# Modulation pieces over two feed-forward groups, and where a chunk's transposes stand

## The chip, the cores and the metric

The kernel runs on one core of one Trainium2 chip. A core has a matrix engine (TensorE, in the profile PE, its weight loads PEld), VectorE (DVE), ScalarE (ACT), GpSimd (POOL) and SyncE (SP), which here issues all DMAs. The metric is the device time of one execution in microseconds (us).

## What the reference computes

Two blocks of layers over 512 tokens of width 1024, all in float32. The first block has two layers; each also carries 256 context tokens, which the second layer (`last` in the kernel) no longer needs as output:

```python
mod = c_act @ w_mod[l] + b_mod[l]        # six rows: sh1, sc1, g1, sh2, sc2, g2; modc for the context
px = (rmsnorm(x, norm1_g[l]) * (1.0 + sc1) + sh1) @ w_in[l] + b_in[l]
...
x = x + g1 * (y_x @ w_out[l])
x = x + g2 * swiglu(rmsnorm(x, norm2_g[l]) * (1.0 + sc2) + sh2, w_gu[l], w_down[l])
```

The second block has two attention layers. After each mixer: `x = layer_norm(ALPHA * x + h)`, then `x = x + sigmoid(x @ ple_w_gate[i]) * (p[i] @ ple_w_proj[i])`.

## The kernel before

**Precision and tiles.** Every large product is made of three matmuls: an operand is split into a rounded part `hi` and a rest `lo`, and hi*hi, hi*lo and lo*hi are summed in PSUM. `wblock` (L154) loads a weight block in two halves into `raw`, copies each to `hi` on ACT and subtracts on DVE for `lo`; `hi` and `lo` have three buffers each, `raw` three. Activations are kept both by token (a chunk is 128 tokens, `xt[c]`) and transposed, features on partitions, as a pair `Hh`, `Hl`.

**A chunk's way into H.** `scaled` (L380) multiplies a chunk by its 1/rms; `finish_T` (L349) makes eight TensorE transposes in two groups of four, applies a scale and a shift per feature (first group on ACT, second on DVE), copies to `Hh` on ACT and subtracts for `Hl` (first group on DVE, second on POOL). `to_T` (L393) does the same without scale and shift, with both subtractions on DVE.

**What sets the order.** The code is one long program; `Pending` (L53) holds functions with a chunk's number as key, so that their instructions are written later than the place where they are added: `keep(n)` runs all but the newest n, `upto(key)` all up to a key. `Lane` (L32) holds generators, `pump(n)` runs n of their steps, `drain` all. When the program is built, a scheduler orders each engine's instructions; the place in the code counts as priority among those that are ready, and a tile's instructions wait for a free buffer of its pool.

**Layer, after the mixer** (L984 to L1005): for each chunk c in turn the output projection in its quarters n = 2 and 3 (48 matmuls of 256 columns), the residual (`resid`), the sum of squares, and with n = 3 the pending list's `keep(1)`, `scaled`, and `finish_T(c)` added to the list. With n = 3 of the last chunk but one the first gate-and-up block gu[0] is loaded, in layer 1 with the last chunk gu[1] too.

**Feed-forward** (L1010 on): 22 blocks of 128 hidden features in groups of 4, 6, 6 and 6. For each block gate and up are 96 matmuls; after a group, its down projection (`wide`, L225) adds to the residual in two halves of 512 columns, each from two weight blocks. Chunks 0 to 3 sum in banks of the PSUM pool "mm" (four), chunk 4 in "md" (one bank), chunk 5 in "tr" (three). Block 0 goes by 256 columns of tokens (`fm_pair`, L196, in layer 0; `fm_pairs`, L206, blocks 0 and 1 in layer 1) and calls `upto` between them, as does the first projection of the second attention (L1635).

**Modulation pieces.** `mod_gen` (L271) computes one of the six rows of `mod` as a generator: four steps that each load 1 MB of `w_mod` into the one buffer `wm` and issue 16 matmuls of 32 weight columns (TensorE rows `md<-wm,cact`), which sum in a bank of "md", and a fifth step that reads the bank (DVE `mb`), and transposes or stores the row. In layer 0 five such generators are added in block 0 (L1035 on): the rows g2 of this layer and sh1, sc1, g1, sc2 of the next; in layer 1 one, g2. Each block pumps 3 steps in layer 0 and 1 in layer 1, and after group 0 the lane is drained.

**After an attention** (`post_attention`, L1293): `wide` with the output weights; in its second half each chunk is finished in turn, normalised, and `finish_T(c)` is added after `keep(1)`. Then `embed_gate` (L1337) runs `wide` with the gate weights, whose `pre` calls `upto(c + 1)` ahead of each chunk's step (L1339). After the first attention its `done_a` (L1609) transposes each finished chunk into HB for the second.

Of the kernel before, what the change touches and what calls it, by code (L numbers as in the profile page):

```python
# [70 lines left out]
def emit(ctx, tc, a, out):  # L71
# [12 lines left out]
    def close(p):  # L84
        p[0].__exit__(None, None, None)
# [68 lines left out]
    def wblock(src, nk, n, into=None):  # L154
        hi, lo = into or (T(wp, [128, nk, n], t, F32R, bufs=3) for t in ("hi", "lo"))
        h = (nk + 1) // 2
        for k0, k1 in ((0, h), (h, nk)):
            raw = T(wp, [128, k1 - k0, n], "raw", bufs=3)
            ld(raw, src[:, k0 * n:k1 * n].rearrange("p (k n) -> p k n", n=n))
            hs = hi[:, k0:k1, :]  # L160
            act(hs, raw, AF.Copy)
            tt(lo[:, k0:k1, :], raw, hs.bitcast(F32), SUB)
        return hi, lo
# [32 lines left out]
    def fm_pair(wb, H, segs):  # L196

        pss = [[mmt()[:, 0:n] for (_, n) in segs] for _ in range(2)]
        for i, (o, n) in enumerate(segs):
            for q in range(0, n, 256):  # L200
                pend.upto((o + q) // 128 + 3)
                for m in range(2):
                    fm_into([pss[m][i][:, q:q + 256]], wb, 128 * m, H, [(o + q, 256)])
        return pss
# [125 lines left out]
    def mcol(l, what, r):  # L330
        t = modc[l][what]
        return lambda kc: t[:, kc % 2, kc // 2, r:r + 1]
# [4 lines left out]
    modl = Lane()  # L337
# [42 lines left out]
    def scaled(pool, xt, rs):  # L380

        h = [T(pool, [128, 512], "xs", bufs=4) for _ in range(2)]
        ts(h[0], xt[:, 0:512], rs, MUL)
        act(h[1], xt[:, 512:1024], AF.Copy, scale=rs)
        return lambda kc: h[kc // 4][:, 128 * (kc % 4):128 * (kc % 4) + 128]
# [486 lines left out]
    def layer(l, H1, hside, oside, x_in, nn, mix_mods, ffn_mods):  # L872
# [111 lines left out]
        for n, c in order:  # L984
                if n not in wbo:
                    wbo[n] = wblock(a["w_out"][l, n], 8, 256)
                if (n, c) == (3, chs[-2]):
                    gu[0] = wblock(a["w_gu"][l, 0], 8, 256)
                if last and (n, c) == (3, chs[-1]):
                    gu[1] = wblock(a["w_gu"][l, 1], 8, 256)  # L990
                wb = wbo[n]
                if n or c >= ne:
                    ps = mmt()[:, 0:256]
                    out_proj((Yh, Yl), wb, c, ps)
                else:
                    ps = early["ps"][:, c, :]
                if n == 3:
                    pend.keep(1)
                resid(OP, c, n, ps, gb[c // 4])
                if n == 0:  # L1000
                    ss[c] = sst()
                sq_part(OP, ss[c], xt[c], n)
                if n == 3:
                    xn = scaled(NP, xt[c], rms(ss[c]))
                    pend.add(c, lambda xn=xn, c=c: finish_T(NP, xn, H2, 128 * c, mcol(l, SC2, c // 4),  # L1005
                                                            mcol(l, SH2, c // 4)))
        close(YP)
        close(OP)

# [3 lines left out]
        for gi, grp in enumerate(GROUPS):  # L1013
            acts = {}
            for jj in grp:
                if jj in gu:
                    wb = gu[jj]
                else:
                    with behind("AV" if jj == 1 else ""):
                        wb = wblock(a["w_gu"][l, jj], 8, 256)  # L1020
                ah = T(FP, [128, TT_], "ah", F32R, bufs=6)
                al = T(FP, [128, TT_], "al", F32R, bufs=6)
                if jj == 0 and last:
                    both = fm_pairs([wb, gu[1]], H2, 2)
                    pg, pu = both[0]
                elif jj == 0:
                    pg, pu = fm_pair(wb, H2, segs)
                elif jj == 1 and last:
                    pg, pu = both[1]
                else:  # L1030
                    pg = fm(wb, 0, H2, segs)
                    pu = fm(wb, 128, H2, segs)
                if jj == 0:
                    close(NP)
                    MP = opened("mp", oside)  # L1035
                    for m in ffn_mods:
                        modl.add(mod_gen(*m, pool=MP))
                modl.pump(1 if last else 3)
                sg = T(FP, [128, TT_], "sg", bufs=2)
                for p, (o, n) in zip(pg, segs):  # L1040
                    act(sg[:, o:o + n], p, AF.Sigmoid)
                    tt(sg[:, o:o + n], p, sg[:, o:o + n], MUL)
                for p, (o, n) in zip(pu, segs):
                    tt(sg[:, o:o + n], p, sg[:, o:o + n], MUL)
                split(ah, al, sg)
                acts[jj] = (ah, al)
            if gi == 0:
                modl.drain()
                close(MP)
                for q in range(1 if last else 2):  # L1050
                    t = T(FP, [128, D], "g2", bufs=2)
                    bcast_row(t, gd[l][1, q])
                    g2.append(t)
            lastg = gi == len(GROUPS) - 1
            if lastg:
                close(H2p)
                H1n = nn["open"](oside, FP)

            def down(c, n2, ps):
                if lastg and n2 == 1:  # L1060
                    pend.keep(1)
                for n in (2 * n2, 2 * n2 + 1):
                    resid(FP, c, n, ps[:, 256 * (n % 2):256 * (n % 2) + 256], g2[c // 4])
                    if lastg:
                        if n == 0:
                            ss[c] = sst()
                        sq_part(FP, ss[c], xt[c], n)
                        if n == 3:
                            nn["chunk"](H1n, c, xt[c], ss[c])

            wide(a["w_d4"][l] if gi == 0 else a["w_d6"][l, gi - 1], len(grp) // 2,
                 lambda c, k: [t[:, 128 * c:128 * c + 128] for t in acts[grp[k]]], chs,
                 lambda c: mmt() if c < 4 else (mdt, trt)[c - 4](), down, by_chunk=lastg)
# [219 lines left out]
    def post_attention(i, Y, w_out, xin, sideh, first=None):  # L1293
        HP = opened("hp", sideh)
        H = halloc(HP, 512)
        PO = opened("po", sideh)
        lg = T(PO, [128, D], "lg")
        lb = T(PO, [128, D], "lb")
        bcast_row(lg, a["ln_g"][i])
        bcast_row(lb, a["ln_b"][i])  # L1300
        xt, bst = {}, {}
        for c in range(4):
            xt[c] = T(w6, [128, D], "w")
            ld(xt[c], xin(c))

        def use(c, n2, ps):
            for n in (2 * n2, 2 * n2 + 1):
                sl = slice(256 * n, 256 * n + 256)
                stt(xt[c][:, sl], xt[c][:, sl], ALPHA, ps[:, 256 * (n % 2):256 * (n % 2) + 256], MUL, ADD)
                if n == 0:  # L1310
                    bst[c] = T(S2, [128, 4, 6], "lst", bufs=4)
                V.bn_stats(out=bst[c][:, n, :], in_=xt[c][:, sl])
                if n == 3:
                    pend.keep(1)
                    mv = T(sm, [128, 2], "mv")
                    V.bn_aggr(out=mv, in_=bst[c])
                    rs = T(sm, [128, 1], "rs")
                    rstd_of(rs, mv[:, 1:2], LN_EPS)
                    nb = T(sm, [128, 1], "nb")
                    stt(nb, mv[:, 0:1], -1.0, rs, MUL, MUL)  # L1320
                    ts(xt[c][:, 0:512], xt[c][:, 0:512], mv[:, 0:1], SUB, rs, MUL)
                    act(xt[c][:, 512:1024], xt[c][:, 512:1024], AF.Identity, scale=rs, bias=nb)
                    pend.add(c, lambda c=c: finish_T(PO, blocks(xt[c]), H, 128 * c, lcol(1 + i), lcol(3 + i)))

        wide(w_out, 4, lambda c, k: [t[:, 128 * c:128 * c + 128] for t in Y[k]], range(4), bank4, use, None, None, first)

        def affine(c):
            with behind("G"):
                tt(xt[c], xt[c], lg, MUL, e=G)
            tt(xt[c], xt[c], lb, ADD)  # L1330

        return HP, H, PO, xt, affine
# [276 lines left out]
    def done_a(c, n, t):  # L1609
        if n == 3:  # L1610
            if not HB:
                HB.extend(T(HBp, [128, 8, 512], t, F32R, bufs=1) for t in ("Hh", "Hl"))
            ld(x4[c], t)
            to_T(lambda kc: t[:, 128 * kc:128 * kc + 128], HB, 128 * c)

    embed_gate(0, H, PO, xt, affine, done_a, early)
    close(PO)
# [270 lines left out]
```

## Time and profile before

| what | value |
|---|---|
| median of 3 runs | 2688.26 us (2686.65 to 2691.68) |
| profiled execution | 2693.03 us |
| its span, first to last instruction | 2691.3 us |
| TensorE busy in the span | 2570.1 us, 95% |
| DVE, ACT, POOL busy | 1330.6, 971.6, 574.2 us |
| mean granted TensorE clock | 0.979 of full speed |

The profiled execution is the one that every row below comes from; its own time is its span and 1.7 us around it. A busy TensorE is not TensorE at its peak, since matmuls overlap in the records. Waits that matter are those of the engine that is busy nearly always, so the stretches to look for are those where TensorE is not.

### The profile page before, as it was taken

Reading aid. Unit: us, or ns where it says so; the run is one execution under the profiler, and the core shown is the slowest. Engines: PE = TensorE matmul, PEld = TensorE weight load, DVE = VectorE, ACT = ScalarE, POOL = GpSimd, SP = SyncE. Lnnn points to the kernel's source line nnn. Section 1 sums busy time; section 2 is a strip of 40 time slices with the busy share of each in tenths; the row PEclk is TensorE's granted clock in tenths of the full one; section 3 lists DMA queues with packets and bytes.
Section 4 is the critical chain, followed back from the end, with each engine's and each line's share of the span. In section 5 each row is a group of like instructions: output and inputs, shape, how many; then the busy total and the mean of one; then the engine's idle time right before and its main releaser. Section 6 shows DMA issues by size and latency. Waiting matters only on the chain.

```text
span 2691.3 us, 39898 instructions
## 1 busy us (share of the span) xinstructions
PE 2570.1 (95%) x15408; PEld 2168.1 (81%) x15408; DVE 1330.6 (49%) x2858; ACT 971.6 (36%) x2034; POOL 574.2 (21%) x614
## 2 busy tenths in 40 slices
PE   7999989859999999999999999999999999989998
PEld 5888788638888888887888888888888888768776
DVE  5675654123232325656634434444454545665666
ACT  3324534012121115344522222433434345434743
POOL 1175531010110204015411211311111211021112
PEclk9999999969999999999999999999999999999999
DMA  8321643541221213225543323343444444524452
GB/s 299 129 71 54 185 157 124 182 147 61 65 68 58 73 53 117 71 78 160 179 132 104 102 85 97 119 119 94 124 126 124 128 122 131 172 86 135 119 165 63
DMA packets 132287, 314.77 MB, mean 117 GB/s; under 512 B 18784, under 2 KB 49088, under 8 KB 132096
## 3 DMA queue, kind: packets, MB, share of 16 engines
q1 hardware_dynamic: 132096, 312.20, 37.0%
q8 instruction: 122, 2.00, 0.3%
q14 instruction: 69, 0.57, 0.1%
HBM read 272.02 MB, written 13.89 MB: 106 GB/s over the span
## 4 chain that ended last, share of the span: by engine, by line
PE 84%; DMA 5%; DVE 4%; ACT 3%; POOL 2%; issue 2%; SPq 0%; DVEq 0%; POOLq 0%; ACTq 0%
PE mm L138 70%; PE md L138 6%; PE tr L138 5%; DMA wm<-in_w_mod_dram 3%; PE tr L1271 1%; POOL w L124 1%; DMA t<-mwd 1%; ACT t L121 1%; DVE lo L124 1%; DVE t L124 1%; ACT hi L121 0%; DVE w L124 0%; DMA g<-gd 0%; POOL t L124 0%; ACT sb L121 0%
## 5 line engine op out<-in xcount | busy, mean ns | idle before, releaser
L138 PE MATMUL mm<-Hh,hi 128*128 128x512 f32 (+1 forms) x2208 | 800.2, 363 | 3.5 <-ACT hi L121 3.3
L138 PE MATMUL mm<-Hl,hi 128*128 128x512 f32 (+1 forms) x2208 | 773.4, 361 | 1.6 <-DVE rv L131 1.3
L138 PE MATMUL mm<-Hh,lo 128*128 128x512 f32 (+1 forms) x2208 | 713.4, 361 | 1.4 <-DVE lo L124 1.4
L121 ACT ACTIVATE hi<-raw 128x1024 fp32r<-128x1024 f32 (+1 forms) x350 | 341.3, 1003 | 826.6 <-PE mm L138 373.1
L124 DVE TENSOR_TENSOR lo<-raw,hi 128x1024 fp32r<-128x1024 f32 (+1 forms) x350 | 426.6, 1232 | 271.0 <-ACT hi L121 270.6
L138 PEld LDWEIGHTS mm<-Hh,hi 128*128 128x128 f32 x2208 | 418.0, 189 | 93.5 <-ACT hi L121 3.8
L138 PEld LDWEIGHTS mm<-Hl,hi 128*128 128x128 f32 x2208 | 418.1, 189 | 65.1 <-DVE rv L131 1.6
L138 PEld LDWEIGHTS mm<-Hh,lo 128*128 128x128 f32 x2208 | 381.7, 189 | 48.0 <-DVE lo L124 2.7
L124 POOL TENSOR_TENSOR w<-w,ot 128x256 f32<-128x256 f32 x200 | 171.4, 881 | 893.8 <-DVE ot L124 891.6
L124 DVE TENSOR_TENSOR sg<-mm,sg 128x512 f32<-128x512 f32 (+1 forms) x132 | 75.7, 599 | 397.8 <-PE mm L138 227.7
L138 PE MATMUL mm<-hi,Hh 128*128 128x256 f32 (+2 forms) x740 | 225.1, 304 | 5.7 <-ACT Hh L121 5.6
L138 PE MATMUL mm<-lo,Hh 128*128 128x256 f32 (+2 forms) x740 | 220.2, 298 | 2.3 <-DVE lo L124 2.3
L138 PE MATMUL mm<-hi,Hl 128*128 128x256 f32 (+2 forms) x740 | 220.7, 298 | 1.0 <-POOL Hl L124 1.0
L124 POOL TENSOR_TENSOR qr<-rt,rt 128x512 f32<-128x512 f32 x58 | 81.7, 1423 | 484.6 <-DVE rt L124 350.5
L138 PEld LDWEIGHTS mm<-hi,Hh 128*128 128x128 f32 x740 | 140.8, 190 | 14.2 <-ACT Hh L121 6.8
L138 PEld LDWEIGHTS mm<-hi,Hl 128*128 128x128 f32 x740 | 140.9, 190 | 7.5 <-DVE Hl L124 1.3
L138 PEld LDWEIGHTS mm<-lo,Hh 128*128 128x128 f32 x740 | 141.0, 191 | 6.4 <-DVE lo L124 2.7
L138 PE MATMUL mm<-hi,ah 128*128 128x512 f32 x352 | 139.9, 397 | 0.0
L138 PE MATMUL mm<-hi,al 128*128 128x512 f32 x352 | 139.5, 396 | 0.0
L138 PE MATMUL mm<-lo,ah 128*128 128x512 f32 x352 | 139.5, 396 | 0.0
L138 PE MATMUL mm<-hi,Yh 128*128 128x256 f32 (+1 forms) x416 | 130.2, 313 | 6.2 <-DVE ot L124 3.7
L138 PE MATMUL mm<-hi,Yl 128*128 128x256 f32 (+1 forms) x416 | 129.0, 310 | 1.5 <-POOL Yl L124 1.5
(368 smaller groups left out, 3679.7 us busy)
## 6 DMA issues: line engine op xcount, KB each, us to landing
raw<-in_w_gu_dram SPq DMA_DIRECT2D x88, 512.0 KB
raw<-in_a_in_dram SPq DMA_DIRECT2D x72, 512.0 KB
wm<-in_w_mod_dram SPq DMA_DIRECT2D x24, 1024.0 KB
raw<-in_w_in_dram SPq DMA_DIRECT2D x40, 512.0 KB
raw<-in_w_mod_dram SPq DMA_DIRECT2D x36, 512.0 KB
raw<-in_w_d_dram SPq DMA_DIRECT2D x24, 512.0 KB
raw<-in_w_d_dram SPq DMA_DIRECT2D x40, 256.0 KB
t<-mwd SPq DMA_DIRECT2D x38, 256.0 KB
```

What stands on the lines that cost most here:

```text
L121: return S.activation(o, i, f, **kw)
L124: return (e or V).tensor_tensor(out=o, in0=x, in1=y, op=op)
L138: lasts["P"] = PE.matmul(o, lhsT=l, rhs=r, start=start, stop=stop, **kw).ins
L1271: PE.transpose(pt[:, 128 * i:128 * i + 128], e, ident)
```

## The change

Seven places: the drain of the modulation lane and the closing of its buffer move from the end of group 0 to the end of group 1, and layer 1 pumps two steps per block instead of one; `fm_pair` and `fm_pairs` flush two chunks (one in `fm_pairs`) fewer at each step; in the output projection's loop `keep(1)` ahead of the residual becomes `keep(0)` behind the sum of squares; layer 1's gu[1] is loaded after that loop; `post_attention` has `keep(0)` for `keep(1)`; `done_a` puts its transposes on the pending list.

```diff
--- before.py
+++ after.py
@@ -198,7 +198,7 @@
         pss = [[mmt()[:, 0:n] for (_, n) in segs] for _ in range(2)]
         for i, (o, n) in enumerate(segs):
             for q in range(0, n, 256):
-                pend.upto((o + q) // 128 + 3)
+                pend.upto((o + q) // 128 + 1)
                 for m in range(2):
                     fm_into([pss[m][i][:, q:q + 256]], wb, 128 * m, H, [(o + q, 256)])
         return pss
@@ -986,24 +986,23 @@
                     wbo[n] = wblock(a["w_out"][l, n], 8, 256)
                 if (n, c) == (3, chs[-2]):
                     gu[0] = wblock(a["w_gu"][l, 0], 8, 256)
-                if last and (n, c) == (3, chs[-1]):
-                    gu[1] = wblock(a["w_gu"][l, 1], 8, 256)
                 wb = wbo[n]
                 if n or c >= ne:
                     ps = mmt()[:, 0:256]
                     out_proj((Yh, Yl), wb, c, ps)
                 else:
                     ps = early["ps"][:, c, :]
-                if n == 3:
-                    pend.keep(1)
                 resid(OP, c, n, ps, gb[c // 4])
                 if n == 0:
                     ss[c] = sst()
                 sq_part(OP, ss[c], xt[c], n)
                 if n == 3:
+                    pend.keep(0)
                     xn = scaled(NP, xt[c], rms(ss[c]))
                     pend.add(c, lambda xn=xn, c=c: finish_T(NP, xn, H2, 128 * c, mcol(l, SC2, c // 4),
                                                             mcol(l, SH2, c // 4)))
+        if last:
+            gu[1] = wblock(a["w_gu"][l, 1], 8, 256)
         close(YP)
         close(OP)
 
@@ -1021,7 +1020,7 @@
                 ah = T(FP, [128, TT_], "ah", F32R, bufs=6)
                 al = T(FP, [128, TT_], "al", F32R, bufs=6)
                 if jj == 0 and last:
-                    both = fm_pairs([wb, gu[1]], H2, 2)
+                    both = fm_pairs([wb, gu[1]], H2, 1)
                     pg, pu = both[0]
                 elif jj == 0:
                     pg, pu = fm_pair(wb, H2, segs)
@@ -1035,7 +1034,7 @@
                     MP = opened("mp", oside)
                     for m in ffn_mods:
                         modl.add(mod_gen(*m, pool=MP))
-                modl.pump(1 if last else 3)
+                modl.pump(2 if last else 3)
                 sg = T(FP, [128, TT_], "sg", bufs=2)
                 for p, (o, n) in zip(pg, segs):
                     act(sg[:, o:o + n], p, AF.Sigmoid)
@@ -1044,9 +1043,10 @@
                     tt(sg[:, o:o + n], p, sg[:, o:o + n], MUL)
                 split(ah, al, sg)
                 acts[jj] = (ah, al)
-            if gi == 0:
+            if gi == 1:
                 modl.drain()
                 close(MP)
+            if gi == 0:
                 for q in range(1 if last else 2):
                     t = T(FP, [128, D], "g2", bufs=2)
                     bcast_row(t, gd[l][1, q])
@@ -1311,7 +1311,7 @@
                     bst[c] = T(S2, [128, 4, 6], "lst", bufs=4)
                 V.bn_stats(out=bst[c][:, n, :], in_=xt[c][:, sl])
                 if n == 3:
-                    pend.keep(1)
+                    pend.keep(0)
                     mv = T(sm, [128, 2], "mv")
                     V.bn_aggr(out=mv, in_=bst[c])
                     rs = T(sm, [128, 1], "rs")
@@ -1611,7 +1611,8 @@
             if not HB:
                 HB.extend(T(HBp, [128, 8, 512], t, F32R, bufs=1) for t in ("Hh", "Hl"))
             ld(x4[c], t)
-            to_T(lambda kc: t[:, 128 * kc:128 * kc + 128], HB, 128 * c)
+            pend.keep(0)
+            pend.add(c, lambda: to_T(blocks(t), HB, 128 * c))
 
     embed_gate(0, H, PO, xt, affine, done_a, early)
     close(PO)
```

## Rows read from the trace of the kernel before

**Rows 1.** The page: span, and busy time of each engine.
```profile
span 2691.3 us, 39898 instructions
...
PE 2570.1 (95%) x15408; PEld 2168.1 (81%) x15408; DVE 1330.6 (49%) x2858; ACT 971.6 (36%) x2034; POOL 574.2 (21%) x614
```

**Rows 2.** Table by stage: stretch, length, busy by engine, clock, DMA share, GB/s.
```profile
440.00:503.00 63.00, 60.08 (x420) 47.61 (x419) 16.29 (x26) 11.38 (x19) 0.00 (x0) 1.00 0.57 194
503.00:526.00 23.00, 20.88 (x122) 14.38 (x120) 5.63 (x14) 0.41 (x1) 5.67 (x8) 1.00 0.55 185
526.00:583.00 57.00, 15.47 (x128) 4.94 (x128) 0.55 (x3) 0.00 (x0) 0.00 (x0) 0.53 0.46 153
...
603.00:712.00 109.00, 109.00 (x616) 95.36 (x616) 33.94 (x47) 21.89 (x32) 5.62 (x6) 1.00 0.20 62
```

**Rows 3.** Timeline of TensorE, 529 to 584 us: start, length, instruction, [idle before <-releaser].
```profile
529.89 1.94 PE L138 MATMUL md<-wm,cact 128*32 128x256 f32 x16 [4.09 <-DMA wm<-in_w_mod_dram]
...
580.89 1.94 PE L138 MATMUL md<-wm,cact 128*32 128x256 f32 x16 [5.30 <-DMA wm<-in_w_mod_dram]
583.37 0.80 PE L138 MATMUL md<-hi,ah 128*128 128x512 f32 x1 [0.55 <-DVE mb L124]
```

**Rows 4.** Timeline of TensorE, 487 to 518 us, modulation pieces.
```profile
487.46 1.07 PE L138 MATMUL md<-wm,cact 128*32 128x256 f32 x16 [0.21 <-DMA wm<-in_w_mod_dram]
...
501.65 1.07 PE L138 MATMUL md<-wm,cact 128*32 128x256 f32 x16
509.01 1.07 PE L138 MATMUL md<-wm,cact 128*32 128x256 f32 x16 [0.74 <-DMA wm<-in_w_mod_dram]
516.72 1.07 PE L138 MATMUL md<-wm,cact 128*32 128x256 f32 x16 [1.08 <-DMA wm<-in_w_mod_dram]
```

**Rows 5.** The chain that ended last, in order of time: start, length, what.
```profile
406.49 5.68 PE mm L138 x48
...
602.41 108.25 PE mm L138 x612
...
714.86 8.40 PE mm L138 x36
```

**Rows 6.** Timelines of TensorE, ACT, DVE and POOL, 425 to 435 us.
```profile
427.08 0.66 PE L354 MATMUL tr<-ident,xs 128*128 128x128 f32 x4
434.52 0.39 PE L138 MATMUL mm<-Hl,hi 128*128 128x256 f32 x1 [0.31 <-POOL Hl L124]
...
425.52 1.50 ACT L121 ACTIVATE t<-tr,modc,modc 128x128 f32<-128x128 f32 x4 [2.58 <-PE tr L354]
...
430.04 0.63 ACT L121 ACTIVATE Hh<-t 128x512 fp32r<-128x512 f32 x1
...
427.72 0.69 DVE L124 TENSOR_TENSOR Hl<-t,Hh 128x512 fp32r<-128x512 f32 x1 [0.32 <-ACT Hh L121]
...
433.18 1.29 POOL L124 TENSOR_TENSOR Hl<-t,Hh 128x512 fp32r<-128x512 f32 x1 [3.60 <-ACT Hh L121]
```

**Rows 7.** Layer 1: table by stage, then timelines of TensorE and DVE.
```profile
1334.00:1352.00 18.00, 12.98 (x81) 12.04 (x81) 11.77 (x19) 9.85 (x21) 5.78 (x5) 0.72 0.41 132
...
1334.54 1.47 PE L354 MATMUL tr<-ident,xs 128*128 128x128 f32 x12
...
1351.11 1.03 PE L354 MATMUL tr<-ident,xs 128*128 128x128 f32 x8
...
1337.41 1.23 DVE L124 TENSOR_TENSOR lo<-raw,hi 128x1024 fp32r<-128x1024 f32 x1 [2.11 <-ACT hi L121]
```

**Rows 8.** After each attention: table by stage, then TensorE's timeline of the first.
```profile
2365.00:2387.00 22.00, 18.00 (x78) 13.45 (x77) 13.62 (x27) 13.15 (x25) 8.37 (x5) 0.92 0.33 96
2632.00:2654.00 22.00, 17.97 (x77) 13.54 (x76) 13.75 (x28) 12.54 (x23) 8.60 (x6) 0.92 0.08 25
...
2374.53 1.09 PE L354 MATMUL tr<-ident,w 128*128 128x128 f32 x8 [1.10 <-DVE w L133]
...
2381.70 0.50 PE L138 MATMUL md<-hi,Hh 128*128 128x512 f32 x1 [1.78 <-ACT Hh L121]
```

**Rows 9.** End of the first gate, timelines of TensorE, ACT and DVE.
```profile
2428.53 0.60 PE L397 MATMUL tr<-ident,w 128*128 128x128 f32 x4
...
2429.27 0.61 ACT L121 ACTIVATE Hh<-tr 128x512 fp32r<-128x512 f32 x1
...
2430.64 0.69 DVE L124 TENSOR_TENSOR Hl<-tr,Hh 128x512 fp32r<-128x512 f32 x1
```

## The prediction

> **What bounds it now.** I read the page first: the span is 2691.3 us and TensorE is busy for 2570.1 us of it [rows 1], so anything worth having lies in stretches where TensorE waits. The table by stage then finds the largest [rows 2]: from 526 to 583 us TensorE has 15.5 us of work in 57, DVE 0.6, ACT and POOL none, and the granted clock is 0.53, near the lower (1.2 GHz) of its two levels, after full clock before it; from 603 to 712 us, one feed-forward group later, it works without a gap at full clock. The timeline names the waits [rows 3]: eight pieces of modulation, each of 16 small matmuls, each behind a 1 MB load of `wm`, with idle times of 4.09 to 5.58 us, 41.5 us in sum (first and last stand there). `wm` has one buffer, so each load starts only when the piece before is through.
>
> Why does nothing else run? The order on an engine is fixed when the kernel is built, and it is not that of the code: what is ready passes what isn't. From 503 to 526 us TensorE has 122 matmuls [rows 2], 48 of pieces, 2 transposes and 72 of the down projection, and those 72 are chunks 0 to 3 of the first half and of the second half's first weight block. What is missing is chunk 4, whose sum goes to the one bank of the pool "md", in which a modulation sums from its first to its last piece. Its first matmul comes at 583.37 us, right after the last piece and DVE's read of that bank [rows 3]. All five modulations stand ahead of it in the code, because the drain does. So the place of the drain, L1047 to L1049, is worth most here.
>
> **A, the drain moved to the second group (layer 0).** Three steps in each of the first four blocks are 12: two modulations of five steps, and two of the third's four loads. The other two loads, and the fourth and fifth modulation (8 loads), now stand behind group 0's down projection. Before, that projection runs from 502.7 us (the last piece ahead of it, 501.65 + 1.07 [rows 4]) to 602.4 us, where block 4's gate and up begin [rows 5]: 99.7 us. After, it holds 144 matmuls at 8.40/36 = 0.233 us [rows 5] = 33.6; pieces two to four of the third modulation, 3 x 1.07 = 3.2, with 0.7 of wait on the second [rows 4]; then chunk 4 still waits for that modulation. TensorE finishes what is ready first, so the third piece, whose load has long landed, is late, and the fourth's load starts behind it: 5.3 of load as in [rows 3] and 0.55 for DVE's read, 5.9. The last weight block's split starts only when chunk 4 is through: 1 more. In all 44.4, so 55.3 saved. Paid later: eight pieces among the 109 us of group 1's blocks at 1.07 = 8.6, and a short wait each. Of the pieces that ran among other matmuls, those that waited did so for 0.21, 0.74 and 1.08 [rows 4], mean 0.68, times 8 = 5.4. A = -55.3 + 14.0 = -41. Ends: no wait at the fourth piece nor in group 1, -53; every one of the eight exposed by 5.2 as now, -5. I take -41, since group 1 has the same neighbours as the stretch from 440 to 503 us, in which TensorE is busy for 60.1 of 63 us with pieces and weights loading together [rows 2].
>
> In that stretch the queue of SP carries both kinds of load at 194 GB/s, and a block's weights still come in time. The Trainium skill (DMA: Bandwidth & Descriptors, Queues, rings and completion order) says that on each DMA engine descriptors are consumed in ring order, so a weight load issued behind a 1 MB piece would wait for all of it; if TensorE felt that at each piece, A would be at its worse end, -5. That is the first rival below; the row speaks against it.
>
> Layer 1 has one modulation (five steps); two steps per block instead of one finish it in block 2. Its four pieces run among blocks 1 to 3 with no idle time today, so 0.
>
> **B, layer 0's last chunk.** The loop now flushes chunk c-1 where it flushed c-2, so one chunk instead of two is pending at its end, and L201 flushes chunk 5 just ahead of the third 256 columns, which need it. Today its transposes go among the second columns and cost 0.31 [rows 6]. After, behind the four transposes of the first half: ACT's four 1.50, its copy 0.6, DVE's subtraction 0.69 [rows 6], 0.3 between them, less 0.5 for the other four transposes: TensorE waits 2.6, with no other bank to fill. The second half, POOL's subtraction in it, ends 6.7 after its transposes today [rows 6]; that is the upper end, nothing the lower. B = +2.3.
>
> **C, layer 1.** From 1334 to 1352 us TensorE is busy for 13.0 of 18 us at a clock of 0.72 [rows 7]; between the two runs of transposes [rows 7], 1336.0 to 1351.1, stand 50 matmuls of 5.68/48 = 0.118 [rows 5] and 4 transposes, 6.4 us of work, so 8.7 are lost, because chunk 1's transposes come late and ACT and DVE split the gate weights ahead of them. After, chunk 1 is through a chunk earlier and the second block's weights are split behind the last chunk's chain. What stays: the first block's second weight half is not split before 1338.64 [rows 7], where TensorE, after 12 matmuls, would want it at 1337.0, 1.6 late; and 2.6 as in B for chunk 3, which is again flushed right ahead of its use. C = -8.7 + 4.2 = -4.5, taken as -4; ends -8 and +4 (6.7 of wait, little gained). The moved `wblock` changes its loads little: they wait for a free buffer, not for their place in the code.
>
> **D, after each attention.** From 2365 us TensorE is idle for 4.0 of 22 us [rows 8]: on the finish of chunk 1, on chunk 3's normalisation (1.10) and on its finish (1.78), and its matmuls are slowed by waits inside a group besides. The stretch from 2632 us does the same, 18.0 busy of 22 [rows 8]. After, chunks 1 and 2 are ready, chunks 0 to 2 of the gate run while chunk 3 is normalised, and its finish meets idle engines: transposes at 2374.5 as now, then 0.6 + 1.5 + 0.6 + 0.7 + 0.3 (B's steps) = 2378.2 where chunk 3's gate now begins at 2381.70 [rows 8], 3.5 sooner, and without the waits inside it. I take 4 each, since chunk 2 is transposed one chunk sooner and its chain may be late by 0.5. D = -8 for both; ends -14 and +1.
>
> **E, the first attention's end.** The edit at L1614 does less than it says: the gate's next step (L1339) flushes chunks 0 to 2 where they stood. Only chunk 3 moves, behind the first columns of `b_k`. Today it has no wait [rows 9]. After: a copy of 0.61 and a subtraction of 0.69 [rows 9] less 0.5, about +1; DVE splits weights there, so +1.5; ends 0 and +3.
>
> Sum: -41 + 2.3 - 4 - 8 + 1.5 = -49. The profiled execution took 2693.0 us; the median of the runs is 2688.3, 4.8 lower. So 2644 for such an execution and **2639** for the median.
>
> **Rivals.**
> 1. The waits go along: the pieces in group 1 stand in TensorE's line with their loads late, and block weights queue behind them. For: one buffer, 5.3 us a load. Against: the stretch 440 to 503. The eight waits stay whole (41.5): A = -5, 2675.
> 2. The bank: the fourth modulation takes "md" before chunk 4's second half does, since its piece is ready first. Then that half waits for four more loads of 7.2 (5.3 and 1.93, [rows 3]) = 29: 2668. Against: today slots go in the code's order, as chunk 4 waits for all five.
> 3. Slower: the drain is only moved. Pieces give way to blocks 4 to 9, and group 1's chunk 4 waits for the bank as group 0's did. It decides if all eight loads are left at block 9; then the 57 us come back at 712, A = 0, B to E at their upper ends (+6, +4, +1, +3): 2702 at the most; +5.4 is passed where the flushed transposes cost over 5.4. Against: eight loads of 7.2 are 58 us, and the blocks last 109.
> 4. The transposes gain nothing (C and D at nought, B and E as above): 2651.
>
> **Numbers.** Forecast 0.78 (own range 2624 to 2656), rival 1 0.05, rival 2 0.06, rival 3 0.05, rival 4 0.06. About 0.2%, 5.4 us, can be told from no change. Rival 3 ends slower in 0.03 and within 0.2% in 0.02, and 0.01 of rival 1, with its waits longer, ends within it too; the rest, 0.94, is faster. The range reaches from 2622, A's better end (-12) and 5 more of D's, to rivals 4 and 2, 2668; rivals 1 and 3 (0.10) and the forecast's tails stay out.
>
> **What would show it.** Right: no stretch of group 0 with DVE empty and the clock near 0.5; chunk 4's first matmul near 535 us and block 4 near 547; eight pieces between 547 and 660 with waits below 1.1; one wait of about 6 ahead of the third modulation's last piece. A wait of 2 to 3 us on ACT's or DVE's finish before the third columns in layer 0 and the second in layer 1. The gate after attention done some 4 us sooner. Wrong: waits of 5 us on `wm` in group 1, or a gap before its down projection.

## The result, and the profile after

The changed kernel takes **2647.05 us** (median of 4 runs, 2644.89 to 2648.58) where the kernel before takes 2689.73 (4 runs): a ratio of 0.9831, 95% interval 0.9816 to 0.9846. The medians are 43 us apart; the ratio stands for 45 (41 to 49). Forecast were 2639 us, in a range of 2622 to 2668, so the measured median lies in the range, 8 us above the forecast. The profiled execution took 2648.43 us, against 2693.03 before.

The page first: span, and busy time by engine.

```profile
span 2646.5 us, 39879 instructions
...
PE 2562.8 (97%) x15408; PEld 2163.4 (82%) x15408; DVE 1326.3 (50%) x2858; ACT 972.0 (37%) x2034; POOL 570.5 (22%) x614
```

Against [rows 1] the same 15408 matmuls stand in a span 44.8 us shorter. TensorE's busy time fell by 7.3 only, so the other 37.5 were idle time. Where they were is seen in the table by stage of the kernel after (columns as in [rows 2]: stretch, length, busy by engine, clock, DMA share, GB/s):

```profile
440.00:503.00 63.00, 60.43 (x415) 47.89 (x414) 15.38 (x24) 10.53 (x16) 0.00 (x0) 0.97 0.59 202
503.00:526.00 23.00, 23.00 (x126) 17.59 (x125) 6.20 (x14) 2.00 (x3) 5.67 (x8) 1.00 0.41 138
526.00:550.00 24.00, 18.33 (x86) 12.94 (x86) 8.33 (x15) 4.34 (x5) 6.75 (x7) 0.79 0.46 150
550.00:660.00 110.00, 109.29 (x700) 90.73 (x700) 35.80 (x53) 21.28 (x30) 10.36 (x10) 1.00 0.41 138
660.00:712.00 52.00, 52.00 (x231) 42.17 (x230) 18.94 (x31) 7.92 (x9) 16.73 (x20) 1.00 0.25 76
```

The stretch of 57 us with 15.5 of work [rows 2] is gone. What is left of it is one gap of 5.7 us between 526 and 550, with the clock at 0.79 in mean. The eight pieces now lie in the 110 us behind it, which TensorE fills to 109.29. Its timeline shows the first bank's handing over and what the pieces wait for:

```profile
513.00 0.40 PE L138 MATMUL tr<-hi,ah 128*128 128x512 f32 x1
...
528.49 1.07 PE L138 MATMUL md<-wm,cact 128*32 128x256 f32 x16
534.69 1.94 PE L138 MATMUL md<-wm,cact 128*32 128x256 f32 x16 [5.12 <-DMA wm<-in_w_mod_dram]
537.17 0.79 PE L138 MATMUL md<-hi,ah 128*128 128x512 f32 x1 [0.55 <-DVE mb L124]
...
544.47 0.39 PE L138 MATMUL md<-hi,ah 128*128 128x512 f32 x1
...
613.33 1.07 PE L138 MATMUL md<-wm,cact 128*32 128x256 f32 x16 [0.42 <-DMA wm<-in_w_mod_dram]
626.10 1.07 PE L138 MATMUL md<-wm,cact 128*32 128x256 f32 x16
632.76 1.07 PE L138 MATMUL md<-wm,cact 128*32 128x256 f32 x16 [0.28 <-DMA wm<-in_w_mod_dram]
```

These are the same work as in [rows 3, 4]. Chunk 4 (`md<-hi,ah`) starts at 537.17 us, behind the third modulation's last piece, instead of 583.37 behind the fifth's; its second half, at 544.47, waits for nothing. Chunk 5 (`tr<-hi,ah`) starts at 513.00. Of the eight moved pieces only two wait, 0.42 and 0.28 us.

The chain of waits gives the landmarks (start, length, what): block 4's gate and up (at 602.41 in the kernel before, [rows 5]), group 2's (752.66 before), the first projection of the second block (1737.69), the first attention's output (2330.40) and what follows its gate (2448.20).

```profile
552.79 16.65 PE mm L138 x96
...
714.11 108.25 PE mm L138 x612
...
1697.10 39.71 PE mm L138 x264
...
2289.93 8.40 PE mm L138 x36
...
2406.13 30.68 PE mm L138 x132
```

The other parts of the change show as new waits of TensorE. Its timeline at layer 0's last chunk (answers to [rows 6]), in layer 1's out-projection and first block [rows 7], and after the first attention [rows 8, 9]:

```profile
434.72 0.51 PE L138 MATMUL mm<-Hh,hi 128*128 128x256 f32 x2 [1.82 <-ACT Hh L121]
435.44 0.38 PE L138 MATMUL mm<-Hl,hi 128*128 128x256 f32 x1 [0.22 <-DVE Hl L124]
...
1272.80 0.39 PE L138 MATMUL mm<-hi,Yh 128*128 128x256 f32 x1 [1.41 <-DVE ot L124]
...
1288.08 1.06 PE L354 MATMUL tr<-ident,xs 128*128 128x128 f32 x8 [1.16 <-DVE xs L131]
...
1315.98 0.73 PE L138 MATMUL mm<-Hh,hi 128*128 128x256 f32 x4 [1.88 <-ACT Hh L121]
...
2336.17 1.09 PE L354 MATMUL tr<-ident,w 128*128 128x128 f32 x8 [2.72 <-DVE w L133]
2339.14 0.50 PE L138 MATMUL md<-hi,Hh 128*128 128x512 f32 x1
...
2366.00 0.69 PE L397 MATMUL tr<-ident,w 128*128 128x128 f32 x2 [5.60 <-DVE w L124]
2392.95 0.74 PE L138 MATMUL mm<-Hh,hi 128*128 128x256 f32 x3 [0.25 <-ACT Hh L121]
```

After the attention the waits of 0.82, 1.10, 0.30 and 1.78 us before chunk 3's gate (sum 4.0; two of them in [rows 8]) became one of 2.72 on its normalisation. Further on, chunk 0's transposes into HB wait 5.60 us for its finished gate (3.71 in the kernel before).

### The profile page after: what moved, and what is told of

Read it like the earlier page. It is cut to its first block, busy times and chain, and to the rows that moved or that the text cites. A ratio compares the mean times of both kernels' runs of the same rounds, so it can differ in the third digit from the quotient of the medians.

```text
span 2646.5 us, 39879 instructions
## 1 busy us (share of the span) xinstructions
PE 2562.8 (97%) x15408; PEld 2163.4 (82%) x15408; DVE 1326.3 (50%) x2858; ACT 972.0 (37%) x2034; POOL 570.5 (22%) x614
## 3 DMA queue, kind: packets, MB, share of 16 engines
q1 hardware_dynamic: 132096, 312.20, 37.5%
## 4 chain that ended last, share of the span: by engine, by line
PE 86%; DMA 4%; DVE 4%; ACT 2%; POOL 2%; issue 1%; SPq 0%; DVEq 0%; POOLq 0%; ACTq 0%
PE mm L138 73%; PE md L138 5%; PE tr L138 5%; PE tr L1271 1%; DMA wm<-in_w_mod_dram 1%; DVE lo L124 1%; POOL w L124 1%; DMA t<-mwd 1%; ACT t L121 1%; PE tr L354 1%; DMA g<-gd 1%; ACT hi L121 1%; DVE t L124 1%; DVE w L124 0%; DMA raw<-in_w_out_dram 0%
```

## The experiments

Twelve kernels were run, in three groups, each on one chip and beside the kernel before on the same chip (2689.66, 2690.99 and 2691.61 us in median). Ratios are to that.

**1. The drain alone.** Into the kernel before:

```diff
-            if gi == 0:
+            if gi == 1:
                 modl.drain()
                 close(MP)
+            if gi == 0:
...
-                modl.pump(1 if last else 3)
+                modl.pump(2 if last else 3)
```

> The kernel before with only the drain and the closing of wm moved to group 1, and two steps per block in layer 1. Theory (the drain carries nearly all of it): the two traces differ by 53.1 us in group 0's down projection and by +11.2 in group 1's blocks, so this run gains about 42 us, to 2647 to 2651 us; its first feed-forward columns have no wait on the last chunk's finish. Rival (the moved transposes carry 10 us or more of the 42.7): 2657 us or more.

Measured: 2648.27 us, ratio 0.9845 [0.9831, 0.9859], 41.7 us less than before. This is nearly the whole gain, and part A's forecast of 41.

**2. Everything but the drain.** The change with drain and pump put back:

```diff
-                modl.pump(2 if last else 3)
+                modl.pump(1 if last else 3)
...
-            if gi == 1:
+            if gi == 0:
                 modl.drain()
                 close(MP)
-            if gi == 0:
```

> The changed kernel with drain and pump as before: the moved transposes alone. Theory: +2.2 in layer 0, -3 in layer 1, -2 and -2.7 after the two attentions, +0.5 at the first attention's end, so -3 to -6 us, 2684 to 2687 us, and the stretch with eight waits on wm is back. Rival (the transposes carry 10 us or more): 2680 us or less.

Measured: 2686.42 us (11 runs), ratio 0.9987 [0.9978, 0.9996], 3.5 us less than before, with 1.1 and 5.9 as ends. Its table by stage has the dead stretch back, against [rows 2]:

```profile
526.00:583.00 57.00, 15.68 (x129) 5.15 (x129) 1.16 (x4) 0.00 (x0) 0.00 (x0) 0.52 0.46 153
```

So the two halves add up within the noise: 41.7 + 3.5 = 45.2, and together 43 (medians) to 45 (ratio) were measured.

**3. The bank, with the drain left where it was.** The rival to "the drain's place" is that eight loads just take their time. Into the kernel before, in layer 0's feed-forward only: "tr" has two banks instead of three, and chunks 4 and 5 sum in a pool of their own with one bank.

```diff
...
+        if not last:
+            psum(4, 2, 1)
...
-                 lambda c: mmt() if c < 4 else (mdt, trt)[c - 4](), down, by_chunk=lastg)
+                 lambda c: mmt() if c < 4 else T(PS["c4"], [128, 512], "c4"), down, by_chunk=lastg)
...
```

> The kernel before, drain at the end of group 0 as it was, but in layer 0's feed-forward the PSUM pool tr has two banks instead of three and chunks 4 and 5 of the down projection sum in the bank so freed, in turn. Theory (what held TensorE was the bank that chunk 4 shares with the modulation, not the drain's place as such): the down projection goes on while the drain's pieces run, the eight waits of 4 to 5.6 us become waits of about 1 us or less, and some 35 to 45 us go, to 2645 to 2655 us; the shared bank may cost up to 3 us in each group. Rival (the pieces stand ahead in the code and one wm buffer feeds them, so TensorE waits whatever the banks): 2685 to 2695 us with the eight waits in place.

Measured: 2646.43 us, ratio 0.9828 [0.9815, 0.9841]: as much as the drain's move gives, with the drain in its old place. Its table by stage and TensorE's timeline (here line 140 is what was line 138):

```profile
503.00:526.00 23.00, 22.77 (x144) 15.88 (x144) 7.78 (x18) 2.23 (x4) 7.05 (x10) 1.00 0.54 183
526.00:590.00 64.00, 60.32 (x395) 46.05 (x394) 22.50 (x37) 11.54 (x15) 11.86 (x14) 1.00 0.66 222
```

```profile
510.81 1.07 PE L140 MATMUL md<-wm,cact 128*32 128x256 f32 x16 [0.23 <-DMA wm<-in_w_mod_dram]
512.14 0.40 PE L140 MATMUL c<-hi,ah 128*128 128x512 f32 x1
...
538.34 1.07 PE L140 MATMUL md<-wm,cact 128*32 128x256 f32 x16 [0.70 <-DMA wm<-in_w_mod_dram]
...
560.57 1.07 PE L140 MATMUL md<-wm,cact 128*32 128x256 f32 x16 [2.16 <-DMA wm<-in_w_mod_dram]
...
581.76 1.07 PE L140 MATMUL md<-wm,cact 128*32 128x256 f32 x16 [0.81 <-DMA wm<-in_w_mod_dram]
```

The same eight loads through the same single `wm` now cost 3.7 us of waits (0.70, 2.16 and 0.81) where it was 41.5: chunk 4 (`c<-hi,ah`) starts at 512.14 us, pieces and blocks run among each other, and the clock stays at 1.00. This shows the cause of the dead stretch: not the loads by themselves, but that the work which could cover them was held by banks that the modulations ahead of it in the code were to have first.

Blocks 4 and on sum in "mm" and need none of these banks; that they could not fill the stretch either is seen in ACT's next split of weights, in the kernel before, the changed one and this one:

```profile
588.43 1.16 ACT L121 ACTIVATE hi<-raw 128x512 fp32r<-128x512 f32 x2 [85.03 <-PE tr L138]
```

```profile
540.13 1.15 ACT L121 ACTIVATE hi<-raw 128x512 fp32r<-128x512 f32 x2 [33.28 <-PE md L138]
```

```profile
525.77 1.15 ACT L123 ACTIVATE hi<-raw 128x512 fp32r<-128x512 f32 x2 [20.07 <-PE c L140]
```

It waits for chunk 5's or chunk 4's matmuls. There are three buffers `hi`, and the first weight block of the down projection keeps its own until chunks 4 and 5 have used it. As I read it, the bank thus held up the last down block's weights and those of group 1 behind them; no run with more `hi` buffers was made.

The Trainium skill (Perfetto Trace Analysis, Optimizing Tensor Performance, Matmuls) asks that independent groups of matmuls rotate through different banks, for the sake of the reading engine; here the trace agrees that a bank shared by independent groups is dear, though the wait for the reader was only 0.55 us (583.37 in [rows 3], 537.17 after the change): what held it was a group that stood unfinished for want of loads.

**4. The one gap that is left, taken away in two ways.** Either two steps fewer in group 0 (3, 3, 2 and 2, so that two whole modulations stand ahead of the down projection and no third one is left half summed in chunk 4's bank), or two buffers `wm`:

```diff
-                modl.pump(2 if last else 3)
+                modl.pump(2 if last or jj in (2, 3) else 3)
```

> The changed kernel with 3, 3, 2 and 2 steps in group 0's four blocks of layer 0, so that two whole modulations stand ahead of the down projection and none is left half summed in the bank that chunk 4 needs. Theory (chunk 4 waits for the bank): the wait of 5.1 us on wm and the 0.55 on DVE ahead of chunk 4 go, with the matmuls that ran at a lower clock after them; 6 to 9 us less, 2638 to 2641 us. Rival (the wait is that of the one wm buffer and only moves into group 1, which now has two more pieces): 2645 to 2648 us, with waits of over 2 us on wm after the down projection.

```diff
-            wm = (T(pool, [128, 2, 1024], "wm", bufs=1) if pool
+            wm = (T(pool, [128, 2, 1024], "wm", bufs=2) if pool
```

> The changed kernel with two wm buffers. Theory (the wait ahead of the third modulation's last piece is one load that can only start when the piece before is through): both loads have landed when TensorE comes to them, the wait of 5.1 us and the one of 2.4 us in group 0 go, 5 to 8 us less, 2639 to 2642 us. Rival (two loads of 1 MB in flight hold up the weight loads queued behind them): waits on raw of over 2 us among the blocks, 2646 us or more.

Measured: 2639.04 us, ratio 0.9809 [0.9793, 0.9824], and 2638.82, 0.9796 [0.9782, 0.981]. By the medians both are 8 us below the changed kernel (by the ratios, 6 and 9), though the wait is 5.67 (5.12 + 0.55). The stretch of the changed kernel's gap in both, by stage, first with the fewer steps, then with two buffers:

```profile
526.00:550.00 24.00, 24.00 (x125) 20.39 (x124) 11.29 (x18) 4.89 (x6) 11.36 (x12) 1.00 0.33 108
```

```profile
526.00:550.00 24.00, 23.45 (x134) 18.38 (x133) 15.08 (x25) 6.50 (x8) 15.27 (x16) 1.00 0.59 200
```

The clock is 1.00 where the changed kernel has 0.79. In the changed kernel the piece behind the wait takes 1.94 instead of 1.07, and chunk 4's 12 matmuls take 5.3 us from 537.17 on instead of 2.8: 3.4 us that follow the wait. 5.7 + 3.4 = 9.1, which is about what disappears.

**5. The lookahead of the first columns.** The change, with the flush in `fm_pair` and `fm_pairs` as before:

```diff
-                pend.upto((o + q) // 128 + 1)
+                pend.upto((o + q) // 128 + 3)
...
-                    both = fm_pairs([wb, gu[1]], H2, 1)
+                    both = fm_pairs([wb, gu[1]], H2, 2)
```

> The changed kernel with fm_pair and fm_pairs flushing as early as before (lookahead 3, first = 2), all else as changed. Theory (a chunk flushed right ahead of its use exposes its finish, 2.0 us in layer 0, 1.9 in layer 1, 0.3 at b_k): those three waits go and the time falls by 3 to 5 us, to 2642 to 2644 us. Rival (the earlier place only moves the wait, because the last chunk's chain is not ready there): 2646 to 2648 us, with a wait on xs in front of the transposes.

Measured: 2643.84 us, ratio 0.983 [0.9816, 0.9844], not told apart from the changed kernel by its interval. TensorE's timeline has no wait at layer 0's last chunk any more, and in layer 1 one on the normalisation instead of on the finish:

```profile
428.30 1.04 PE L354 MATMUL tr<-ident,xs 128*128 128x128 f32 x8
...
1303.41 1.09 PE L354 MATMUL tr<-ident,xs 128*128 128x128 f32 x8 [1.84 <-DVE xs L131]
```

So by its trace this edit costs the change the 2.0 us of layer 0's waits (the 0.31 before them was less), while the ratio can't tell it. Together with the ten steps of experiment 4:

> The changed kernel with early flushes (as e3_flush_early) and ten steps in group 0 (as e4_ten_steps). Theory (the two cures act in different stretches): the gains add, 3.2 + 8 = 11 us less than the changed kernel, 2634 to 2638 us. Rival (the earlier start of block 0's successors meets wm or weight loads that are late): 2639 us or more.

Measured: 2635.22 us, ratio 0.9793 [0.978, 0.9807], where the ten steps alone have 0.9809. The median is 11.8 us below the changed kernel's, as a sum of the two would be (11); the intervals of the two ratios overlap.

**6. What holds the first gate.** The chain of the changed kernel comes to chunk 0's late transposes (2366.00, 5.60) over the gate's product and the load of the tile `pq` that it is multiplied with:

```profile
2343.36 5.75 DVE w L124 x2
2350.04 4.55 DVE w L124 x2
...
2359.55 0.49 DVE pg L124 x2
2360.05 4.68 DMA pq<-pp
2367.54 5.12 PE mm L138 x18
```

`pq` has four buffers, so a load waits until the product four quarters earlier is through: the load at 2360.05 starts as the product before it ends. With seven:

```diff
-                p = T(PO, [128, 256], "pq", bufs=4)
+                p = T(PO, [128, 256], "pq", bufs=7)
```

> The changed kernel with seven buffers for the gate's pq loads instead of four. Theory (after the first attention the chunk's finish came 3.6 us sooner, but TensorE then waits 5.6 instead of 3.7 us for chunk 0's result, on a pq load that waits for a buffer): 1 to 3 us less, 2644 to 2646 us, with that wait shorter. Rival (POOL's multiplication and DVE's addition in affine set it, whatever the loads): 2646 to 2648 us, the wait of 5.6 us unchanged.

Measured: 2641.54 us, ratio 0.9813 [0.9799, 0.9826]. That is 5.5 us below the changed kernel by the medians, more than the 1 to 3 expected. The timeline's wait is halved, the first stays:

```profile
2337.27 1.09 PE L354 MATMUL tr<-ident,w 128*128 128x128 f32 x8 [2.72 <-DVE w L133]
2364.41 0.44 PE L397 MATMUL tr<-ident,w 128*128 128x128 f32 x2 [2.91 <-DVE w L124]
```

**7. The edit after the attentions, undone alone**, and the changed kernel once more beside it:

```diff
-                    pend.keep(0)
+                    pend.keep(1)
```

> The change with one place undone: post_attention keeps one chunk pending, as before. Theory (the place is what saved the time after each attention, 2.0 and 2.7 us by the landmarks, and the lost part is only what chunk 3's normalisation gave back): +4 to +5, about 2652 us, with chunk 3's gate after the first attention again 17 us behind its output projection instead of 13.7. Rival (the gate is held by the normalisation's chain and the loads of pq, whatever is pending): within 1.5 us of the changed kernel, 2646 to 2649 us.

> The changed kernel itself, with nothing altered, so that the three runs beside it have it on the same chip. Both theories expect what it took before: a ratio of 0.983 to the kernel before, about 2647 us, within 2 us.

Measured: 2651.64 us, ratio 0.9854 [0.984, 0.9867], and 2647.7, 0.984 [0.9824, 0.9856]. The medians differ by 3.9, near the theory's 4 to 5, and the four runs of the first (2651.22 and more) lie above all but one of the changed kernel's nine on both chips (the others are at most 2648.58); the intervals overlap. The traces show less. At the same matmul of layer 0's block 0 (437.87 and 434.24 us) they differ by 3.6 us already, and up to there the two kernels are the same. The stages themselves stand in this table, from the chain's landmarks in every trace (x264, x36 and x132 as in the chain above; traces with a further edit in a stage are left out of its row):

| stage, us | transposes as before | as changed | difference |
|---|---|---|---|
| group 2 to x264 (has layer 1, C) | 985.03, 985.07 | 980.78 to 982.99, mean of 7: 982.3 | -2.7 |
| x36 to x132 (first attention's end, D and E) | 116.78 to 118.04, mean of 4: 117.4 | 115.38 to 117.84, mean of 7: 116.3 | -1.1 |
| the second stage with seven `pq` | | 111.35 to 114.03, mean of 3: 112.4 | -3.9 to "as changed" |
| x132 to the end (second attention, D) | 240.61 to 243.10, mean of 4: 241.4 | 239.19 to 240.89, mean of 10: 240.3 | -1.0 |

In the second row one of the four "as before" (118.04, this experiment) has E as changed. In the last row "as before" hangs on one trace: without the 243.10 its mean is 240.8, and the difference 0.5. One execution each of the kernel before and the changed one would have given 1.6 and 2.7 for the two rows with D; over all the traces it is about 1 each. So D is some 2 by the stages and some 4 by the medians of this experiment. Which is nearer stays open; both are at most half of what the prediction gave it.

**8. All together.** The change with experiments 4 (steps), 5 and 6, without and with two buffers `wm`:

> The change with three further edits at once: the lookahead of the first feed-forward columns as before, ten steps of modulation in the first group's last two blocks, seven buffers for the products pq of the gate. If the three sit in different stretches and add up, -3.2, -8 and -3 to -5 from the changed kernel: 2631 to 2633 us. If the third only fills a wait that the finished chunks would have filled anyway, 2635 us, as without it.

> As the run before, with two buffers wm for the modulation's loads besides. If ten steps and two buffers remove the same wait (the one ahead of the third modulation's last piece), nothing is left for the second: within 1 us of the run before. If the single buffer also delays the block weights by its loads (2.4 us ahead of the first group's second block in the changed kernel's trace), 2 us less.

Measured: **2629.86 us**, ratio 0.9771 [0.9758, 0.9785], and **2624.54**, 0.9751 [0.9734, 0.9768]. The three edits add up (18 us from the changed kernel on the same chip, a little more than the 14 to 17 expected). What the second `wm` adds stays open: its median is 5 lower, but its four runs lie between 2619.6 and 2628.9, and the profiled one, the slowest of these, has a span 0.7 us shorter than without (2627.1 to 2627.8). Both beat the changed kernel.

## Why the prediction was right, and which of its terms were not

**A, right in sum and in mechanism.** Forecast -41; the drain alone measured -41.7, and in the profiled pair the end of group 1's blocks moved from 710.7 to 672.1 us, 38.5 sooner, although group 0's down projection began 3.4 later (2.2 of that is part B): -41.9. Its two halves were each 2 to 3 off. Saved: the down projection lasts from 506.10 to 552.63, 46.5 us instead of 99.6, so 53.1 where 55.3 were forecast. The wait itself was as worked out, 5.12 + 0.55 against 5.9; the miss is the clock behind it, which the sum took as full although [rows 2, 3] show it low behind such waits: 3.4 us. Paid: group 1 up to its down projection's end grew by 11 us instead of 14: the eight pieces wait 0.7 in all where 5.4 were taken (the mean of the three waits seen, for all eight), while 1.8 that the sum did not have came in beside the pieces' own 8.6. Of the signs named, chunk 4 came at 537 us (535 named) and block 4 at 552.6 (547 named).

**Rival 1** (the waits go along) fell: two short waits and 109.29 busy of 110. The queue's ring order, which the Trainium skill states (DMA: Bandwidth & Descriptors, Queues, rings and completion order), may have held weights behind pieces there; TensorE didn't feel it. **Rival 2** (the fourth modulation takes the bank first) fell: 544.47 without a wait. Here too the bank went in the code's order. **Rival 3** (slower) fell: the last moved piece is through at 640.3 us, before block 9, and 660 to 712 us has TensorE busy throughout. **Rival 4** (the transposes gain nothing) was near: parts B to E are worth 3.5 us, not the forecast's 8.2 nor rival 4's loss of 3.8. Its 2651 lies even nearer to the measured median than the 2639, but by its number only.

**A reading that was incomplete.** The prediction named chunk 4 alone as missing before 526 us. Chunk 5 was missing too: it sums in a bank of "tr", and came at 586.52, behind the last drained modulation's transposes into "tr" (583.96). After the change it starts at 513.00. That changes no term, as the sum counted all 144 matmuls. I take it for the same cause in a second pool; no run moved chunk 5 alone.

**B, right**: +2.3 forecast; 1.82 + 0.22 of wait in place of 0.31, and the end of the first block moved by +2.2.

**C, a little too large**: -4 forecast, -2.7 in the table of stages. The late finish of chunk 1 is gone, and in its place came waits that the sum did not have: 1.41 and 1.16 in the out-projection's loop, on DVE, where a chunk's normalisation and its neighbour's residual now meet (that is my reading of the two releasers; no run took them apart). A slip in its sum is small: 12 matmuls of 0.118 from 1336.0 us end at 1337.4, not 1337.0, so the 1.6 late should be 1.2.

**D, the failed term**: -8 for both, measured some -2 by the stages (at most -4 by experiment 7's medians). The step that failed is "transposes at 2374.5 as now". From the start of the attention's output (x36) to chunk 3's transposes, the kernel with `keep(1)` takes 2335.09 - 2290.85 = 44.2 us, the changed one 2336.17 - 2289.93 = 46.2. The rows of the former, chain and timeline:

```profile
2290.85 8.40 PE mm L138 x36
```

```profile
2335.09 1.10 PE L354 MATMUL tr<-ident,w 128*128 128x128 f32 x8 [1.10 <-DVE w L133]
2336.49 0.50 PE L138 MATMUL mm<-hi,Hh 128*128 128x512 f32 x1 [0.30 <-ACT Hh L121]
2342.27 0.50 PE L138 MATMUL md<-hi,Hh 128*128 128x512 f32 x1 [1.76 <-ACT Hh L121]
```

From the transposes to chunk 3's gate it takes 7.2 us here, 3.0 in the changed kernel (2336.17 to 2339.14): 4.2 saved where 3.5 were forecast. But 2.0 are lost ahead: chunk 1's transposes, 1.1, now stand before the projection's end instead of behind it, and chunk 3's normalisation on DVE ends 0.9 later behind that end besides. And three matmuls of the gate that ran before chunk 3's now run after them, 0.7. That leaves 1.5, and 1.3 is the difference of the waits (4.0 to 2.72). In the first attention the wait on chunk 0's gate takes 0.3 of that again (5.60 against 5.28). The shift is not one trace's chance: behind x36, chunk 3's transposes come at 44.1 to 44.2 us and its gate at 51.3 to 51.4 in all four traces with `keep(1)`; at 46.2 to 46.3 and 49.1 to 49.2 in the ten with `keep(0)`, but for one gate at 50.5. The slow matmuls that the prediction put down to waits inside a group were mostly the clock's: behind the wait of 1.78 us chunk 3's matmuls take 0.63 us each in the kernel before, and 0.40 behind 1.76 in the one with `keep(1)`. The landmark of the forecast was thus right ("the gate 4 us sooner" against the projection's end: 13.7 us instead of 17.0), and the gain behind it wasn't: work had only changed sides of the landmark.

**E**: +1.5 forecast; the wait is 0.25.

In sum, -49 forecast and -45 measured in the profiled pair: A and E each 1 better than forecast, B as forecast, C and D together some 7 too good. That A's two halves missed in opposite ways, and A and E made up for some of C and D, was luck. The other 3.4 of the 8 us to the forecast's 2639 come from the step to the median: it took 4.8 off, and the changed kernel's profiled execution lies 1.4 above its median.

## What to carry to other kernels

When TensorE waits on a row of loads and there is other work, ask which bank that work sums in and who stands ahead of it in the code for the same bank: a bank of its own, or a later place of the other user, was worth 42 to 45 us here, with the loads as they were. When a step is moved across a landmark, count the work that changes sides with it before a shorter distance to the landmark is taken as gain. For effects of 1 to 3 us, compare one stage over many traces: two executions of the same kernel differ by as much.

## What the runs showed that was not expected

**The clock behind a short wait isn't the same in each execution.** Chunk 3's gate in the second attention, behind the same wait, in the kernel before and in the one with `keep(1)` in place, by stage:

```profile
2648.50:2653.33 4.83, 4.83 (x14) 3.85 (x15) 0.99 (x2) 0.63 (x1) 3.10 (x2) 0.65 0.01 3
```

```profile
2609.16:2612.47 3.31, 3.31 (x14) 2.63 (x15) 1.00 (x2) 0.63 (x1) 1.57 (x2) 1.00 0.02 5
```

The two kernels have the same work here. After idle times of 1.79 and 1.78 us the same 14 matmuls took 4.83 us at a clock of 0.65 and 3.31 at 1.00. The Trainium skill (TensorE: Matmul & The Clock Gate, Part 1: The HAM clock gate) says that the number of matmuls run at the lower clock differs between runs of one kernel; these rows agree, at 1.5 us for one wait. That is as large as what part D is worth in one attention, and 1.5 of the 2.7 us that the one pair of traces showed for the second.

**A load's wait varies too.** The second modulation piece of layer 0 waits 2.44 us in the profiled execution of the changed kernel, and 0.49 in the other one; TensorE's timeline of the latter:

```profile
447.79 1.07 PE L138 MATMUL md<-wm,cact 128*32 128x256 f32 x16 [0.49 <-DMA wm<-in_w_mod_dram]
```
